# The way down of two chunks as seven block products over pairs of rows, with the third chunk first and in two parts

## The chip, the cores and the metric

The kernel runs on one core of one Trainium2 chip. Its time is the device time of one execution, in microseconds; a kernel is run several times and the median counts. One execution is also recorded by the hardware profiler. Engines are named as in the profile: PE is TensorE (PEld its weight loads), DVE is VectorE, ACT is ScalarE, POOL is GpSimd, SP is the engine that issues nearly all DMAs.

## The reference, cut to what matters

One layer of a streaming encoder, on 1024 + 128 = 1152 tokens of width 1024. The two feed-forward blocks (SwiGLU, inner width 2816) are what the change touches.

```python
def swiglu(x, w_gate, w_up, w_down):
    return (jax.nn.silu(x @ w_gate) * (x @ w_up)) @ w_down

def layer(x, ...):
    x = x + 0.5 * swiglu(rms_norm(x, norm_ffn1), w_ffn1_gate, w_ffn1_up, w_ffn1_down)
    m, ... = mixer(rms_norm(x, norm_mix), ...)      # gated DeltaNet heads and pooling heads, projected
    x = x + m
    x = x + 0.5 * swiglu(rms_norm(x, norm_ffn2), w_ffn2_gate, w_ffn2_up, w_ffn2_down)
    return x, ...
# after the layer: y = rms_norm(x, norm_final)
```

The data are float32. The kernel splits each operand of a large product into a high part (`float32r`) and a low part, so that one product takes three matmuls: high by high, high by low, low by high.

## The kernel before, in words

Tokens lie in the free dimension and features in the 128 partitions. There are three chunks of tokens: chunk 0 with 512, chunks 1 and 2 with 320 each. A feed-forward block is a `half_step` (gate and up) followed by `downs` (the way down). Between the two blocks stands the mixer, whose pieces of work are put in order by a list of names.

**gate_up.** A row `f` is one of the 22 blocks of 128 in the inner width. Chunk 0 takes plain products, 48 matmuls of 512 columns a row. Chunks 1 and 2 are taken together: gate and up are two block rows, the two halves of the width are the inner blocks, the two chunks are two block columns, and this 2 x 2 by 2 x 2 product is made from seven block products (B11, B21, T1, T2, T3, T4, B22) instead of eight, 84 matmuls of 320 columns a row. The sums of weights are made on POOL (`piece`, L314 and L318), a piece is cast on ACT (L319) and its low part made on DVE (L320). Pieces go round a ring of seven buffers, O0 to O6. The sums of activations are made once, by `operands`, into B0 to B6. There are three loops: for the first `AHEAD` = 9 rows chunk 0 goes alone, while the operands are made; rows 9 to 21 take all three chunks (the main loop); last, the first 9 rows are made up for chunks 1 and 2 (the last loop). Each row's result is split into two parts by `keep` (L337, L338) and written to `g_keep0`, `g_keep1` or `g_keep2` in DRAM.

**The way down.** `downs` takes the chunks in the order 1, 0, 2. A `Down` reads the 22 rows of its chunk back into A, B and x tiles (`fetch`, L618), and walks over units: one output block `d` of eight, with up to eight rows. A unit's weights are read into one of three R buffers (L171), cast (L182) and given a low part (L183) in one of three pairs of O buffers; each row is then three matmuls (L55) into PSUM. When all 22 rows of an output are in, DVE adds half of the sum to x (L534). In the second block, the final norm of chunk 1 runs beside chunk 0's way down, that of chunk 0 beside chunk 2's, and that of chunk 2 stands at the end: squares (L1362, L1368), two small sets of matmuls with a power on POOL between (L228, L229), a scaling on DVE or POOL (L1384, L1382), and the write of y (L1385).

**What sets the order.** The framework schedules instructions onto each engine's queue by the order in which they are written and by when it expects their operands and buffers to be ready; an instruction written later can so be put ahead. At run time each engine works through its queue in that fixed order and waits on semaphores. A buffer is named by a tag, and a new tile of a tag waits until the last use of the one before it. Reads of rows are put in a list (`pending`) and go out behind a weight read, so many at a time (`pace`), or all at once (`rest`).

Of the kernel before, what the change touches and what calls it, by code (L numbers as in the profile page):

```python
# [13 lines left out]
P = 128  # L14
# [10 lines left out]
CHUNKS = [(0, 512), (512, 320), (832, 320)]  # L25
HIST = 15
# [11 lines left out]
def trunk(ctx: ExitStack, tc: tile.TileContext, xin, s0, convst, poolst, cm_in, vec_in, small_in,  # L38
# [219 lines left out]

    STEPS = "B11 B21 T2 T1 T3 T4 B22".split()
    N = CHUNKS[1][1]  # L260
    N0 = CHUNKS[0][1]

    def operands(wi, op):
# [19 lines left out]
        split("B11", l1)  # L283
        V.tensor_sub(l1, l1, r1)
        yield
        split("T1", l1)
        yield
        split("B21", l2)
        V.tensor_sub(r1, r2, r1)
        yield  # L290
        split("B22", r2)
        yield
        V.scalar_tensor_tensor(r2, l1, -1.0, r2, ALU.mult, ALU.subtract)
        split("T2", r2)
        yield
        split("T3", r1)
        yield
        V.scalar_tensor_tensor(l2, r2, -1.0, l2, ALU.mult, ALU.subtract)
        split("T4", l2)
        yield  # L300

    def gate_up(wi, wg, wu, gk, H, RB, cs, ahead, norm, x0=None):


        gs, ring = Slots(), [0]

        def piece(*src, more=None):

            t = region(f"O{ring[0] % 7}", F32R)
            ring[0] += 1  # L310
            hi, lo = t[:, :512], t[:, 512:]
            if len(src) == 2:
                t = gs.get("s", 512)
                G.tensor_add(t, *src)  # L314
                src = [t]
            src = src[0]
            if more:
                G.tensor_add(more[0], src, more[1])  # L318
            A.copy(hi, src)  # L319
            V.tensor_sub(lo, src, hi.bitcast(F32))  # L320
            return [x.rearrange("p (k c) -> p k c", k=4) for x in (hi, lo)]

        def product(ps, w, hs, start=True, stop=True):
            for k in range(4):
                (whi, wlo), (hhi, hlo) = w, hs
                T.matmul(ps, whi[:, k, :], hhi[k], start=start and k == 0, stop=False, skip_group_check=True)
                T.matmul(ps, whi[:, k, :], hlo[k], start=False, stop=False, skip_group_check=True)
                T.matmul(ps, wlo[:, k, :], hhi[k], start=False, stop=stop and k == 3, skip_group_check=True)
# [7 lines left out]
        def keep(f, c, go, src):  # L336
            A.copy(go[:, 0], src)  # L337
            G.tensor_sub(go[:, 1], src, go[:, 0].bitcast(F32))  # L338
            SY.dma_start(gk[c][f].rearrange("p (s n) -> p s n", s=2), go.bitcast(F32))
# [3 lines left out]
        def gated0(f, pg, pu):  # L343
# [7 lines left out]
            keep(f, 0, go, sg)  # L351
            yield

        def temps():
            gs.place(region("x10"), ("p1", N, 2), ("c2", N, 2))
            gs.place(region("x11"), ("c3", N, 2), ("sum", 512, 1))
            for i in range(2):
                gs.place(region(f"x2{i}", F32R), ("go1", 2 * N, 1), ("go2", 2 * N, 1))

# [29 lines left out]
        def right_up(f, al, g1, u1, c2, c3):  # L389
# [4 lines left out]
            keep(f, 2, gs.get("go2", 2, N), c2)  # L394

        def left_up(f, al, w4, p1):
# [3 lines left out]
            keep(f, 1, gs.get("go1", 2, N), p1)  # L400
# [65 lines left out]
        for f in range(ahead, NF):  # L466
# [8 lines left out]
            next(done)  # L475
            c2 = right_gate(al, sm, g2, c3)
            product(pu, piece(u1), H0[0], True, False)
            right_up(f, al, g1, u1, c2, c3)
            w4 = piece(u2)
            product(pu, w4, H0[1], False, True)  # L480
            next(done)
            left_up(f, al, w4, p1)
# [4 lines left out]
        for f in range(ahead):  # L487
# [6 lines left out]
            if last:  # L494
                left_up(last[0], last[1], piece(last[2]), last[3])
            c2 = right_gate(al, sm, g2, c3)
            if f + 1 < ahead:
# [3 lines left out]
            last = f, al, u2, p1  # L501
        left_up(last[0], last[1], piece(last[2]), last[3])

    class Down:

        def __init__(self, c, wd, home):
            self.c, self.home = c, home
            fs = list(home)  # L510
            cuts = [(i, fs[i:i + 8]) for i in range(0, NF, 8)]

            self.units = []
            for ds in [(0, 1)] + [(d,) for d in range(2, KT)]:
                self.units += [(d, *cut) for cut in cuts for d in ds]
            self.next = ((wd[d], cut) for d, _, cut in self.units)
            self.raw = [fetch_unit(*next(self.next), 0) for _ in W["raws"]]

        def run(self, beside, done, most=1):
            c, home, ps = self.c, self.home, {}  # L520
            n = CHUNKS[c][1]
            beside = iter(beside)
            for d, at, cut in self.units:
                whi, wlo = split_unit(self.raw.pop(0))
                for src in self.next:
                    self.raw.append(fetch_unit(*src, most))
                    break
                if d not in ps:
                    ps[d] = pt("d")[:, :n]
                for i, f in enumerate(cut):  # L530
                    mm3(ps[d], whi[:, i, :], wlo[:, i, :], home[f][:, :n], home[f][:, n:], at + i == 0, at + i == NF - 1)
                next(beside, None)
                if at + len(cut) == NF:
                    V.scalar_tensor_tensor(xk(c, d), ps[d], 0.5, xk(c, d), ALU.mult, ALU.add)  # L534
                    if done:
                        done(d)
            for _ in beside:
                pass

    SPLITS = (("O1", "O2"), ("O3", "O4"), ("O5", "O6"))  # L540

    AHEAD = 9

    def half_step(wi, wg, wu, gk):
# [30 lines left out]
        rows = list(range(AHEAD, NF)) + list(range(AHEAD))  # L575
        fetch(1, gk, rows[:18], *[f"A{i}" for i in range(6)])
        for _ in run:
            pass
        fetch(1, gk, rows[18:], "A6", "B0")

    def downs(wd, gk, src, done=lambda c: None, after=lambda c: ()):
        weights(("R1", "R2", "R0"), SPLITS)
        rows = list(range(NF))
        d1 = Down(1, wd, homes[1])
        x_new(1)
        fetch_x(1, src)
        rest()
        fetch(0, gk, rows[:14], *[f"B{i}" for i in range(1, 7)], "x20", "x21")
        d1.run((), done(1))
        rest()  # L590
        fetch(0, gk, rows[14:], "A0", "A1", "A2", "A3")
        d0 = Down(0, wd, homes[0])
        fetch(2, gk, rows[:4], "B0")
        d0.run(after(1), done(0), 2)
        rest()
        fetch(2, gk, rows[4:], "B1", "B2", "B3", "B4", "B5")
        d2 = Down(2, wd, homes[2])
        x_new(2)
        fetch_x(2, src)
        for _ in range(4):  # L600
            pending.pop(0)()
        d2.run(after(0), done(2), 4)
        for _ in after(2):
            pass
# [3 lines left out]
    def fetch(c, gk, rows, *where):  # L608
# [4 lines left out]
        for tag in where:  # L613
            t = region(tag, F32R)
            for i in range(min(SIZE[tag] // n, len(left))):
                f = left.pop(0)
                out[f] = t[:, i * n:(i + 1) * n]
                pending.append(lambda f=f: SY.dma_start(out[f].bitcast(F32), gk[c][f]))  # L618
# [16 lines left out]
    weights(("R1", "R0", "O0"), SPLITS)  # L635
# [587 lines left out]
    rstd_of(0, pair(mt("raw", 512), mt("raw", 512), mt("Xs", 512)), R[0], False)  # L1223
# [129 lines left out]
    nt = Slots()  # L1353
    nt.place(region("Q"), ("nacc", 512, 1), ("nsq", 512, 1), ("r", 512, 2))
    squares = {}

    def square(c):

        def add(d):
            n = CHUNKS[c][1]  # L1360
            t = nt.get("nsq" if d else "nacc", n)
            A.activation(t, xk(c, d), AF.Square)  # L1362
            if not d:
                squares[c] = t
            elif c == 2 and d == KT - 1:
                squares[c] = [squares[c], t]
            else:
                V.tensor_add(squares[c], squares[c], t)  # L1368
        return add

    def final(c):
        o, n = CHUNKS[c]
        r = nt.get("r", n)
        last = c == 2
        pool = (2, 5) if last else (1, 4, 7)
        pr = yield from rstd_rest(n, squares[c], r)
        yield
        for k in range(KT):
# [7 lines left out]
            if not last:  # L1386
                yield

    downs(wd2, g_keep, x_keep, square, final)
# [90 lines left out]
```

## Time and profile before

| | |
|---|---|
| median of 3 runs | 2207.68 us (2204.58 to 2208.64) |
| profiled execution: time, and span from first to last instruction | 2208.91 us, 2207.1 us |
| granted clock of TensorE, mean | 0.996 |
| busy: PE / PEld / DVE / ACT / POOL | 98% / 89% / 60% / 41% / 28% |
| moved by DMA | 297.83 MB, 135 GB/s on the mean |
| first gate_up, first way down, mixer | about 0 to 527, 527 to 802, 802 to 1402 us |
| second gate_up, second way down, end | about 1402 to 1915, 1915 to 2194, 2194 to 2207 us |

In the profile's groups a line is one kind of instruction at one line of the kernel: engine, operation, tiles written and read, count, then busy time and mean duration, then the idle time of the engine just before and what ended it. "PEld" rows show weight loads, one for each matmul; as they overlap matmuls, a run of them without a break means that TensorE had work all along. A row of a window gives its length, then the busy time of each engine (with the count of instructions), the granted clock, the share of time in which the 16 DMA engines were busy and the rate.

### The profile page before, as it was taken

To read this page: it belongs to the slowest core of one execution; us is meant where nothing else is said; L and a number is where in the kernel's file an instruction comes from. 1 tells how busy PE (TensorE), PEld (TensorE's weight loads), DVE (VectorE), ACT (ScalarE), POOL (GpSimd) and SP (SyncE) were. 2 spreads that over 40 slices of the span, in tenths; PEclk is the share of its full clock that TensorE was granted. 3 is DMA by queue.
4 is the path that set the end of the run, shared out by engine and by line. 5 is a ranking of instruction groups with operands and counts; after the bars stand their busy time and mean duration, and the time that the engine had idled before them with its cause. 6 is when DMAs were issued, how large, how long until landed. Compare 5 with 4: busy or idle time off the path is not lost.

```text
span 2207.1 us, 32969 instructions
## 1 busy us (share of the span) xinstructions
PE 2155.4 (98%) x12599; PEld 1955.0 (89%) x12599; DVE 1333.2 (60%) x2329; ACT 909.1 (41%) x1726; POOL 614.5 (28%) x556
## 2 busy tenths in 40 slices
PE   8999999999999999999999998999999999999998
PEld 7899999999988987777989887888999999998898
DVE  7855555675423457778677867875555567543243
ACT  6433333453322345545544443543333345432232
POOL 1343443552000002322232333133434445300010
PEclk9999999999999999999999999999999999999999
DMA  6422232467753732122222123442322346676383
GB/s 250 143 94 88 91 112 91 153 197 270 245 188 118 249 110 62 51 65 58 86 63 80 44 92 92 136 151 89 108 87 91 113 144 188 226 259 225 95 291 103
DMA packets 103534, 297.83 MB, mean 135 GB/s; under 512 B 16336, under 2 KB 22352, under 8 KB 103120
## 3 DMA queue, kind: packets, MB, share of 16 engines
q1 hardware_dynamic: 103088, 295.40, 40.7%
q8 instruction: 99, 1.62, 0.3%
q14 instruction: 59, 0.48, 0.1%
q10 hardware_dynamic: 288, 0.33, 0.0%
HBM read 231.54 MB, written 64.14 MB: 134 GB/s over the span
## 4 chain that ended last, share of the span: by engine, by line
PE 86%; DVE 7%; issue 4%; ACT 1%; POOL 1%; DMA 1%; SPq 0%; DVEq 0%; ACTq 0%; POOLq 0%
PE ps_d L55 30%; PE ps_a L55 26%; PE ps_b L55 18%; PE ps_c L55 12%; DVE B L798 1%; DVE A L938 1%; DVE A L1140 1%; PE ps_b L59 1%; DVE A L937 1%; DVE O L183 0%; DMA R<-in_wd 0%; ACT O L182 0%; DVE B L941 0%; DVE R L935 0%; POOL A L1000 0%
## 5 line engine op out<-in xcount | busy, mean ns | idle before, releaser
L55 PE MATMUL ps_d<-B,O 128*128 128x320 f32 (+1 forms) x2784 | 503.6, 334 | 6.0 <-DVE x L819 3.0
L55 PEld LDWEIGHTS ps_d<-B,O 128*128 128x128 f32 x2784 | 441.5, 188 | 39.2 <-DVE x L819 5.2
L55 PE MATMUL ps_a<-A,O 128*128 128x512 f32 (+1 forms) x1712 | 390.8, 363 | 2.1 <-DVE A L938 1.6
L55 PE MATMUL ps_a<-B,O 128*128 128x320 f32 x2272 | 383.3, 309 | 0.0
L183 DVE TENSOR_TENSOR O<-R,O 128x1024 fp32r<-128x1024 f32 (+1 forms) x170 | 195.3, 1149 | 280.2 <-ACT O L182 276.2
L55 PEld LDWEIGHTS ps_a<-B,O 128*128 128x128 f32 x2272 | 348.6, 188 | 6.5 <-issue 0.2
L182 ACT CAST O<-R 128x1024 fp32r<-128x1024 f32 (+1 forms) x182 | 180.6, 993 | 403.9 <-PE ps_d L55 309.0
L55 PEld LDWEIGHTS ps_a<-A,O 128*128 128x128 f32 x1712 | 296.8, 191 | 37.9 <-issue 3.3
L320 DVE TENSOR_TENSOR O<-Q,O 128x512 fp32r<-128x512 f32 x180 | 156.9, 873 | 174.5 <-ACT O L319 174.4
L55 PE MATMUL ps_b<-A,O 128*128 128x512 f32 x1056 | 252.3, 393 | 7.2 <-ACT O L319 7.2
L55 PE MATMUL ps_d<-A,O 128*128 128x320 f32 (+1 forms) x1392 | 241.0, 331 | 1.0 <-DVE x L534 0.9
L55 PEld LDWEIGHTS ps_b<-A,O 128*128 128x128 f32 x1056 | 198.0, 189 | 47.0 <-ACT O L319 7.2
L55 PEld LDWEIGHTS ps_d<-A,O 128*128 128x128 f32 x1392 | 220.6, 188 | 16.4 <-issue 1.2
L320 DVE TENSOR_TENSOR O<-R,O 128x512 fp32r<-128x512 f32 x182 | 172.8, 952 | 34.6 <-ACT O L319 34.2
L319 ACT CAST O<-Q 128x512 fp32r<-128x512 f32 x180 | 111.3, 619 | 165.0 <-PE ps_b L55 66.9
L319 ACT CAST O<-R 128x512 fp32r<-128x512 f32 x182 | 112.3, 620 | 126.4 <-PE ps_a L55 64.3
L55 PE MATMUL ps_c<-A,O 128*128 128x512 f32 x624 | 151.2, 391 | 0.0
L55 PEld LDWEIGHTS ps_c<-A,O 128*128 128x128 f32 x624 | 115.0, 188 | 21.5
L338 POOL TENSOR_TENSOR x<-x,x 128x320 fp32r<-128x320 f32 x88 | 101.7, 1155 | 68.2 <-ACT x L337 65.9
L338 POOL TENSOR_TENSOR A<-A,A 128x512 fp32r<-128x512 f32 x44 | 72.2, 1640 | 122.0 <-ACT A L337 122.0
L314 POOL TENSOR_TENSOR Q<-R 128x512 f32<-128x512 f32 x36 | 51.5, 1430 | 162.1 <-DVE O L320 152.6
L229 POOL TENSOR_TENSOR rt<-rt,vec 128x3 f32<-128x3 f32 (+1 forms) x11 | 13.2, 1202 | 299.1 <-DVE rt L228 299.1
(282 smaller groups left out, 2705.6 us busy)
## 6 DMA issues: line engine op xcount, KB each, us to landing
R<-in_wd SPq DMA_DIRECT2D x80, 512.0 KB, 3.7
g_keep<-x SPq DMA_DIRECT2D x88, 320.0 KB, 2.3
R<-in_wu SPq DMA_DIRECT2D x49, 512.0 KB, 3.7
R<-in_wg SPq DMA_DIRECT2D x48, 512.0 KB, 4.1
g_keep<-A SPq DMA_DIRECT2D x44, 512.0 KB, 2.7
R<-in_wd SPq DMA_DIRECT2D x48, 384.0 KB, 3.7
B<-g_keep SPq DMA_DIRECT2D x46, 320.0 KB, 5.4
A<-g_keep SPq DMA_DIRECT2D x42, 320.0 KB, 4.2
```

The costliest lines, as they stand in the source:

```text
L55: self.put(nc.tensor.matmul(out, lhs, rhs, **k), n / 2400 + .003 if lhs.dtype == F32R else max(n, lhs.shape[-1]) / 600)
L59: self.put(nc.tensor.transpose(out, lhs, rhs), out.shape[-1] / 1200)
L182: A.copy(hi, raw)
L183: (e or V).tensor_sub(lo, raw, hi.bitcast(F32))
L314: G.tensor_add(t, *src)
L319: A.copy(hi, src)
L320: V.tensor_sub(lo, src, hi.bitcast(F32))
L338: G.tensor_sub(go[:, 1], src, go[:, 0].bitcast(F32))
L798: V.scalar_tensor_tensor(y[:, :512], raw[:, t:t + 512], cw[:, t:t + 1], y[:, :512], ALU.mult, ALU.add)
L937: V.tensor_tensor(tu[:, :n, :w], xrow(slice(None), m), Uc[:, :, m:m + 1].to_broadcast([P, n, w]), ALU.mult)
L938: V.tensor_tensor(Uc[:, :, m + 1:], Uc[:, :, m + 1:], tu[:, :n, :w], ALU.add)
L1140: V.tensor_tensor(buf[:, :, :have], cur[:, :, w_:w_ + have], cur[:, :, :have], ALU.add)
```

## The change

Chunks 1 and 2 now go down together, by the seven products that gate_up uses. An output pair is `d` and `d + 4` (two block rows), a pair of rows gives the two inner blocks, and the chunks are the two block columns. The 22 rows are 11 pairs in three groups of 4, 3 and 4 pairs; `ORDER` lays the weights out so that a group's even rows stand together, and then its odd ones. A unit of the new loop `down12` is a group and one of four output pairs: 12 units, numbered 0 to 11, with four weight blocks a11, a12, a21, a22 each. Each unit's partial results are added to x directly: five additions from PSUM on DVE, and two (p1, c3) by way of a copy on ACT and an addition on POOL. Weights come into four buffers (R0, R1, O5, O6), and pieces go round five (O3, O4, O0, O1, O2).

The operands (the right-hand sums) are made where the rows come from. In gate_up, rows from `AHEAD` = 8 on are collected in pairs; `combine` makes the four sums and seven splits of a pair and writes them to `g_keep2`. The first eight rows are written as they are to `g_keep1`; `downs` reads them back and makes their operands (group 0's, into B0 to B6) beside chunk 0's way down.

Chunk 0 goes first (`down0`), in two parts: all eight outputs over its first 14 rows, which are read during gate_up's last loop, and then over the other 8. The first and the last two outputs of each part are taken row by row together. The final norm of chunk 0 runs beside `down12`; those of chunks 1 and 2 both stand at the end. The numbers of some buffers change with this, in the mixer as well.

```diff
+GROUPS = [(0, 4), (4, 3), (7, 4)]
+ORDER = [2 * i + j for p, n in GROUPS for j in range(2) for i in range(p, p + n)]
...
+    def combine(l1, l2, r1, r2, put):
+        put("B11", l1)
+        V.tensor_sub(l1, l1, r1)
+        put("T1", l1)
+        put("B21", l2)
+        V.tensor_sub(r1, r2, r1)
+        put("B22", r2)
+        V.scalar_tensor_tensor(r2, l1, -1.0, r2, ALU.mult, ALU.subtract)
+        put("T2", r2)
+        put("T3", r1)
+        V.scalar_tensor_tensor(l2, r2, -1.0, l2, ALU.mult, ALU.subtract)
+        put("T4", l2)
...
+        def gated(f, c, t):
+            q, i = f // 2, 2 * (c - 1) + f % 2
+            if f < ahead:
+                SY.dma_start(gk[1][q][:, i * N:(i + 1) * N], t)
+                return
+            rows.setdefault(q, {})[i] = t
+            if len(rows[q]) < 4:
+                return
+            def put(name, src):
+                j = DOWN.index(name)
+                go = gs.get("go", 2, N)
+                A.copy(go[:, 0], src)
+                (V if name[0] == "B" else G).tensor_sub(go[:, 1], src, go[:, 0].bitcast(F32))
+                SY.dma_start(gk[2][q - ahead // 2][j].rearrange("p (s n) -> p s n", s=2), go.bitcast(F32))
+            sums.append(combine(*[rows[q][i] for i in range(4)], put))
...
+    def down12(wd, gk, op0, beside, done):
+        bl = Blocks(["O3", "O4", "O0", "O1", "O2"])
+        for tag in ("R0", "R1", "O5", "O6"):
+            gs.place(region(tag), ("raw", 1024, 1))
...
+        def fifth(g, d, w):
+            be, sm, c3 = pt("c")[:, :N], gs.get("sum", w[0].shape[-1]), gs.get("c3", N)
+            product(be, piece(w[2], w[3], more=(sm, w[0])), ops[g]["T1"], True, False)
+            A.mul(c3, be, -0.5)
+            G.tensor_add(xk(2, d + 4), xk(2, d + 4), c3)
+            return be, sm
...
+        ask(1, ["A5", "A0", "A1", "A2", "A3", "A4", "A6"])
+        for u, (g, d) in enumerate(units):
...
+            product(al, piece(a11), op["B11"])
+            A.mul(p1, al, 0.5)
+            G.tensor_add(xk(1, d), xk(1, d), p1)
+            product(ga, piece(a12), op["B21"])
+            if last:
+                left_low(*last)
+            if u == 4:
+                ask(2, [f"B{i}" for i in range(7)])
+            product(al, piece(sm), op["T2"], False)
+            add(1, d, ga)
+            add(2, d, al)
+            product(be, piece(sm, a12), op["B22"], False)
+            add(2, d, be)
+            if u + 1 < len(units):
...
+                w = load(g2, d2, 6 if g2 == 0 else 10)
+                nxt = w, fifth(g2, d2, w)
+            product(al, piece(a11, a21), op["T3"], False)
+            add(2, d + 4, al, -0.5)
...
-    AHEAD = 9
+    AHEAD = 8
...
-        fetch(1, gk, rows[:18], *[f"A{i}" for i in range(6)])
+        fetch(0, gk[0], ORDER[:14], *[f"A{i}" for i in range(7)])
...
+        down0(wd, [(home, first, 0), (second, ask, 2)], sums(), done0)
         rest()
-        d2.run(after(0), done(2), 4)
-        for _ in after(2):
-            pass
+        down12(wd, gk, op0, iter(after(0)), done12)
+        ends = [iter(after(c)) for c in (2, 1)]
```

In this cut some `yield` lines, the calls of the work beside (`next(beside, None)`) and of `ended` are left out. `ask(g, tags)` puts the reads of a group's operands on the list of pending reads; `load(g, d, most)` reads a unit's weights and lets `most` of the pending reads go behind them; `left_low` is the seventh product, T4, which is made one unit later.

More of the change, by code (lines that the diff above doesn't have):

```diff
@@ L282, in operands @@
                     yield
[L283 to L300, printed above, removed]
-    def gate_up(wi, wg, wu, gk, H, RB, cs, ahead, norm, x0=None):
[L305 to L328, printed above, removed]
+        yield from combine(l1, l2, r1, r2, split)
+    def gate_up(wi, wg, wu, gk, H, RB, cs, ahead, norm, x0=None):
+        bl = Blocks([f"O{i}" for i in range(7)])
+        gs, piece, product = bl.gs, bl.piece, bl.product
         def load(f, most=1):
@@ L350, in gated0 @@
             V.tensor_mul(sg, sg, su)
-            keep(f, 0, go, sg)
+            A.copy(go[:, 0], sg)
+            G.tensor_sub(go[:, 1], sg, go[:, 0].bitcast(F32))
+            SY.dma_start(gk[0][f].rearrange("p (s n) -> p s n", s=2), go.bitcast(F32))
             yield
         def temps():
[L355 to L358, printed above, removed]
+            gs.place(region("x10"), ("p1", N, 4))
+            gs.place(region("x11"), ("c2", N, 4))
+            gs.place(region("x20", F32R), ("go", 2 * N, 2))
+            gs.place(region("x21"), ("c3", N, 2), ("sum", 512, 1))
         def fifth(w):
@@ L393, in right_up @@
             V.tensor_mul(c2, c2, c3)
[L394 removed]
+            gated(f, 2, c2)
         def left_up(f, al, w4, p1):
@@ L501, in gate_up, with down0 @@
             last = f, al, u2, p1
+            step()
         left_up(last[0], last[1], piece(last[2]), last[3])
-    class Down:
-        def __init__(self, c, wd, home):
-            self.c, self.home = c, home
+    def down0(wd, parts, beside, done):
+        weights(("R0", "R1", "R2"), (("O4", "O5"), ("O6", "O0"), ("O1", "O2")))
+        units = []
+        for j, (home, ask, most) in enumerate(parts):
             fs = list(home)
[L511 to L531, printed above, removed]
@@ new lines, in down0, with more @@
+            at = sum(len(p[0]) for p in parts[:j])
+            cuts = [(i, fs[i:i + 8]) for i in range(0, len(fs), 8)]
+            for d in range(0, KT, 2):
+                pair = (d, d + 1)
+                both = d in (0, KT - 2)
+                us = [(e, i, cut) for i, cut in cuts for e in pair] if both else [(e, i, cut) for e in pair for i, cut in cuts]
+                units += [(j, e, at + i, i, cut, both) for e, i, cut in us]
+        todo = iter(units)
+        def more(most):
+            for j, d, o, i, cut, both in todo:
+                raw.append(fetch_unit(wd[d][:, o * P:(o + len(cut)) * P], most=most))
+                return
@@ new lines, in down0 @@
+        raw, ps, now = [], {}, -1
+        for _ in W["raws"]:
+            more(0)
+        left = list(units)
+        while left:
+            u = [left.pop(0)]
+            j, d, o, i, cut, both = u[0]
+            if both:
+                u.append(left.pop(0))
+            if j != now:
+                parts[j][1]()
+                now = j
+            home, _, most = parts[j]
+            ws = {}
+            for _, d, *_ in u:
+                ws[d] = split_unit(raw.pop(0))
+                more(most)
+                if i == 0:
+                    ps[d] = pt("d")[:, :N0]
+            for k, f in enumerate(cut):
+                for d, (whi, wlo) in ws.items():
+                    mm3(ps[d], whi[:, k, :], wlo[:, k, :], home[f][:, :N0], home[f][:, N0:], i + k == 0, i + k == len(home) - 1)
+            for d in ws:
@@ L532, in run @@
                 next(beside, None)
-                if at + len(cut) == NF:
-                    V.scalar_tensor_tensor(xk(c, d), ps[d], 0.5, xk(c, d), ALU.mult, ALU.add)
-                    if done:
+                next(beside, None)
+                if i + len(cut) == len(home):
+                    V.scalar_tensor_tensor(xk(0, d), ps[d], 0.5, xk(0, d), ALU.mult, ALU.add)
+                    if j == len(parts) - 1 and done:
                         done(d)
-            for _ in beside:
-                pass
@@ new lines, in downs, with first, sums, put @@
+    def downs(wd, gk, src, done0=None, after=lambda c: (), done12=None):
+        op0, stage = {}, []
+        def first():
+            for q in range(AHEAD // 2):
+                t = region(f"x{1 + q // 2}{q % 2}")
+                SY.dma_start(t, gk[1][q])
+                stage.append([t[:, i * N:(i + 1) * N] for i in range(4)])
+            for i, name in enumerate(DOWN):
+                t = region(f"B{i}", F32R)
+                op0[name] = [[t[:, (2 * k + s) * N:(2 * k + s + 1) * N] for k in range(4)] for s in range(2)]
+        def sums():
+            for q in range(AHEAD // 2):
+                def put(name, src):
+                    hi, lo = [op0[name][s][q] for s in range(2)]
+                    A.copy(hi, src)
+                    V.tensor_sub(lo, src, hi.bitcast(F32))
+                yield from combine(*stage[q], put)
+        home = dict(homes[0])
+        homes.clear()
+        second = {f: None for f in ORDER[14:]}
+        def ask():
+            fetch(0, gk[0], ORDER[14:], "A0", "A1", "A2", "A3")
+            second.update(homes[0])
+            rest()
+            for c in (1, 2):
+                x_new(c)
+                fetch_x(c, src)
+        down0(wd, [(home, first, 0), (second, ask, 2)], sums(), done0)
+        rest()
+        down12(wd, gk, op0, iter(after(0)), done12)
+        ends = [iter(after(c)) for c in (2, 1)]
+        while ends:
+            ends = [e for e in ends if next(e, e) is not e]
```

185 lines of the change are left out of this document (133 added, 52 removed).

## The prediction

> **What bounds the kernel now.** I read the page first, then busy times by stage, then the order in time of TensorE's weight loads.
>
> ```profile
> span 2207.1 us, 32969 instructions
> PE 2155.4 (98%) x12599; PEld 1955.0 (89%) x12599; DVE 1333.2 (60%) x2329; ACT 909.1 (41%) x1726; POOL 614.5 (28%) x556
> PE 86%; DVE 7%; issue 4%; ACT 1%; POOL 1%; DMA 1%; SPq 0%; DVEq 0%; ACTq 0%; POOLq 0%
> ```
>
> The chain of waits lies on TensorE for 86% of the span. A busy PE alone proves little, since ends of matmuls are modelled, so I look at the stages which the change touches:
>
> ```profile
> core 0: us, PE busy (x) PEld busy (x) DVE busy (x) ACT busy (x) POOL busy (x), PEclk, DMA share, GB/s
> 120.00:410.00 290.00, 290.00 (x1645) 265.57 (x1644) 159.10 (x212) 106.61 (x199) 117.67 (x86) 1.00 0.29 95
> 430.00:515.00 85.00, 85.00 (x582) 85.00 (x581) 63.37 (x92) 46.25 (x91) 47.39 (x39) 1.00 0.58 184
> 526.80:802.20 275.40, 274.38 (x1582) 253.30 (x1581) 104.58 (x118) 82.41 (x94) 2.21 (x4) 1.00 0.62 207
> 1914.90:2194.40 279.50, 277.68 (x1609) 256.25 (x1609) 112.64 (x126) 84.08 (x103) 12.47 (x10) 1.00 0.62 209
> ```
>
> The rows are the main loop of the first gate_up (all three chunks), its last loop (chunks 1 and 2 by seven products), and the two ways down. TensorE is without a gap in the first two and has 1 to 2 us of gaps in each of the last two, at a granted clock of 1.00. So matmuls taken out of the ways down shorten the kernel one for one, as long as the new loop is fed. The price of one:
>
> ```profile
> 724.67 77.56 PEld L55 LDWEIGHTS ps_d<-B,O 128*128 128x128 f32 x528
> 1484.76 5.44 PE ps_a L55 x24
> 547.00 9.24 PEld L55 LDWEIGHTS ps_d<-A,O 128*128 128x128 f32 x63 [1.16 <-issue]
> 547.03 9.48 PE L55 MATMUL ps_d<-A,O 128*128 128x320 f32 x63 [0.93 <-DVE x L534]
> 2140.17 54.26 PEld L55 LDWEIGHTS ps_d<-B,O 128*128 128x128 f32 x370 [2.09 <-DVE O L183]
> ```
>
> The whole way down of chunk 2 is one unbroken run: 77.56/528 = 0.147 us for a matmul of 320 columns. With 512 columns it is 5.44/24 = 0.227. The last three rows are the main stalls of the ways down, 1.2 us in the first, 2.1 in the second.
>
> **The change part by part.** *Matmuls.* Chunks 1 and 2 cost 2 x 8 x 22 x 3 = 1056 matmuls in each way down; seven products for 4 output pairs over 11 row pairs cost 7 x 4 x 11 x 3 = 924. Chunk 0 keeps its 528. Over both ways 264 go: 264 x 0.147 = **-38.8 us**. gate_up keeps its matmuls; only the split of rows between its loops moves (8 and 14 for 9 and 13).
>
> *Feeding the new loop.* One unit (a group and an output pair) has 84 matmuls, 12.3 us; the 3-pair group has 63, 9.3 us. Its other work has the shapes of gate_up's last loop:
>
> ```profile
> L320 DVE TENSOR_TENSOR O<-Q,O 128x512 fp32r<-128x512 f32 x26 | 21.9, 843 | 10.8 <-ACT O L319 10.8
> L319 ACT CAST O<-Q 128x512 fp32r<-128x512 f32 x25 | 15.5, 619 | 13.8 <-PE ps_d L55 7.7 <-PE ps_a L55 5.4 <-PE ps_b L55 0.7
> L314 POOL TENSOR_TENSOR Q<-x,R 128x512 f32<-128x512 f32 x4 | 5.2, 1302 | 2.8 <-DVE O L320 2.8
> L338 POOL TENSOR_TENSOR x<-x,x 128x320 fp32r<-128x320 f32 x14 | 12.4, 883 | 17.1 <-ACT x L337 17.1
> L399 DVE SCALAR_TENSOR_TENSOR x<-ps_a,x 128x320 f32<-128x320 f32 x7 | 3.3, 477 | 0.0
> L364 ACT ACTIVATE x<-ps_c 128x320 f32<-128x320 f32 x7 | 3.1, 438 | 5.0 <-PE ps_c L55 5.0
> L393 DVE TENSOR_TENSOR x<-x,x 128x320 f32<-128x320 f32 x7 | 8.4, 1194 | 0.2
> ```
>
> DVE: 7 low parts x 0.84 + 5 additions from PSUM x 0.48 = 8.3 us of 12.3. ACT: 7 x 0.62 + 2 x 0.44 = 5.2. POOL: 4 sums x 1.30 + 2 additions x 0.88 = 7.0. gate_up's last loop carries 75%, 54% and 56% on these engines (row 430 to 515) and TensorE waits nowhere. The one thing that is tighter here is the ring of split pieces, 5 buffers for 7: a piece can be made once the product five before it ended, so four products, 7.0 us, cover a cast, a low part and the sum ahead of them (2.8 us). I take **+2** for both ways, from 0 to 12 (0.07 us for each of 168 products).
>
> *DMA.* Weights fall from 72 to 48 units a way, of up to 512 KB for the old and two of 384 or 512 KB for the new. The operands come as 49 reads of 320 KB and 4 of 640 KB in place of 44 rows. What matters is when: group 2's 28 operands (9.2 MB) go into the B tiles that group 0 frees, so between the starts of units 4 and 8, with the weights of units 5 to 8 (3.4 MB) between them on SP's one queue. That is 12.6 MB.
>
> ```profile
> 540.00:570.00 30.00, 28.98 (x197) 28.48 (x196) 12.88 (x14) 9.63 (x10) 0.00 (x0) 1.00 1.01 381
> 600.00:620.00 20.00, 20.00 (x103) 17.44 (x102) 6.54 (x9) 4.85 (x7) 0.00 (x0) 1.00 0.88 316
> R<-in_wd SPq DMA_DIRECT2D x80, 512.0 KB, 3.7
> g_keep<-x SPq DMA_DIRECT2D x88, 320.0 KB, 2.3
> ```
>
> With a full queue 381 GB/s went through, so the 12.6 MB take 33 us. Unit 8's first product starts 3 x 9.3 + 5 x 1.3 = 34 us after unit 4 and wants its weights 2.8 us earlier, at 31.5, and the weight reads stand behind ten operand reads each. If the first of them waits 1 us for its slot, TensorE loses about 2.5 us: **+5** for both, from 0 to 17 (at the 316 GB/s of the second row 40 us are needed, 8.4 a way late). "DMA: Bandwidth & Descriptors" of the Trainium skill (Specifications) gives a core about 358 GB/s of HBM. The trace went above that, at 381, and the measurement decides; by 358 the estimate of the term would be about +9 and the sum 4 us higher.
>
> *The start of the new loop.* Unit 1's weights go into O5 and O6, and O6 is free only when chunk 0 ends; the reads (3.7 us in flight), two POOL sums and a split then stand against 5 products, 8.8 us. **+1** for both, 0 to 8. Should SP keep the written order at the start of a way, chunk 0's fourth weight unit would queue behind the four 640 KB reads, which wait for gate_up's last row to be written (2.3 us): some 4 us a way.
>
> ```profile
> 517.86 0.42 SPq L174 DMA_DIRECT2D O<-in_win  x1
> 523.06 0.44 SPq L618 DMA_DIRECT2D B<-g_keep  x1
> ```
>
> It does not keep it: a weight of the mixer, written far behind, went out ahead of this way's rows, since its buffer was free. I cost that at nothing; the first two units (16 x 3 x 0.227 = 10.9 us) are the cover.
>
> *Chunk 0 in two parts.* 8 more PSUM evacuations on DVE cost nothing by themselves; 104.58 us in 275.40 leave room, also for 16 additions and 28 splits of the first group's operands. But pairs of outputs now run row by row together and end 0.7 us apart, where both PSUM buffers are wanted at once: three such edges a way. The one of before cost 0.93 (row 547.03); I take 0.3 each, **+2** for both ways, 0 to 5.5.
>
> *gate_up's sums.* For every two rows 4 additions and 3 low parts come onto DVE, at the 1.19 of L393 at worst 8.4 us in 46.6; it had 159.10 in 290.00, 55%, and comes to 73%, as the last loop has with TensorE full. ACT gets 1.5 casts a row. Cover is there; **+1**, 0 to 8.
>
> *Stalls that go.* The three rows above: **-2.5**, 0 to -3.6.
>
> *The end.* Now two chunks of 320 finish together:
>
> ```profile
> 2194.74 0.49 DVE L534 SCALAR_TENSOR_TENSOR x<-ps_d,x 128x320 f32<-128x320 f32 x1 [7.60 <-PE ps_d L55]
> 2200.50 2.84 DVE L1384 SCALAR_TENSOR_TENSOR x<-x,vec,ps_d 128x320 f32<-128x320 f32 x6 [3.19 <-ACT Q L234]
> 2201.08 3.13 SPq L1385 DMA_DIRECT2D out_y<-x  x6
> ```
>
> Six more scalings and six more writes on SP, 3.1 us, less the 1.8 us of chunk 1's last product, which runs when chunk 2 is done: 1.3; I take **+2**, 1.3 to 5. The mixer's start keeps its cover: A0 to A3 are free one group (49 us) ahead.
>
> *Sum.* -38.8 + 2 + 5 + 1 + 2 + 1 - 2.5 + 2 = -28.3. The profiled execution took 2208.91 (its span and 1.8 around it), so 2180.6; it lies 1.2 above the median of the runs, from which I get 2179.4. **Forecast 2180.**
>
> **The rivals.** *The queue takes part of the gain.* Group 1 runs at the speed of its reads: that term at +17 and the start at +4 give 2180 + 12 + 3 = 2195. For it: one queue, ten reads ahead of each weight; share 1.01 at such times before. Against: the shortage is one stage of 37 us.
>
> *Evacuations ahead of pieces (slower).* In a unit an addition that waits for product k's end is written ahead of the low part of product k+1, on the same DVE. Were that the order on the engine, five products of seven would wait 0.48 + 0.84 less the two matmuls that need no low part (0.29), 1.0 us: 120 products, +124 us, 2304. Queued behind would be the next low parts, and TensorE for them. It decides from 28/120 = 0.24 us a product. Against: gate_up's last loop is written alike and shows 85.00 of 85.00. For: 5 buffers let the engines run less far ahead.
>
> *DVE and POOL block each other (slower).* Each low part (0.68 by itself, 0.84 on the mean) would wait for a whole POOL sum of 1.30: 7 x 2.0 + 2.4 = 16.4 us, DVE the bound, about +4 in 24 units, 2276. This is the exclusive lock on the shared port that "SBUF — State Buffer" of the Trainium skill (Who interferes with whom) states. Against: gate_up's last loop has the same mix, so what blocking there is lies in its means already; the rows show how little, 0.92 beside a POOL sum and 0.68 without.
>
> ```profile
> 448.64 1.30 POOL L318 TENSOR_TENSOR x<-Q,R 128x512 f32<-128x512 f32 x1 [1.12 <-issue]
> 449.57 0.92 DVE L320 TENSOR_TENSOR O<-Q,O 128x512 fp32r<-128x512 f32 x1 [0.22 <-ACT O L319]
> 454.13 0.68 DVE L320 TENSOR_TENSOR O<-Q,O 128x512 fp32r<-128x512 f32 x1
> ```
>
> *The change does not do what it says in time.* gate_up's additions hold up its low parts by 1 us a row, 28 rows in both main loops: what the ways down gain is given back, 2208. Against: 73%.
>
> **How the numbers follow.** Forecast (2168 to 2188) 0.63; the queue (2188 to 2203) 0.20; given back 0.04; evacuations 0.10; port 0.03. Under 0.2%, 4.4 us, no difference can be told. Faster 0.63 + 0.20 = 0.83, same 0.04, slower 0.13. The lowest sum of the terms is -38.8 + 1.3 - 3.6 = -41, 2168; the upper end takes in the queue's rival, 2203.
>
> **What would show it.** 924 matmuls of 320 columns between chunk 0's end and the end of each way, at 0.147 each: about 136 us. TensorE's gaps there name the wait: DMA of R or O from in_wd before units 6 to 8 is the queue, DVE with O is the order of evacuations, low parts above 1.2 us on the mean the port. gate_up's rows should still take 85.00 in 85.00 and 290.00 in 290.00. The forecast is wrong if gaps of the new loop exceed 15 us a way, or if gate_up or the mixer's start grows by more than 10.

## The result

The changed kernel takes 2213.28 us (median of 7 runs, 2211.89 to 2218.47) against 2207.68 before (7 runs, 2204.02 to 2208.91): 1.0032 times as long, 95% interval 1.0020 to 1.0043. Slower by 0.3%, where 2180 was forecast. The profiled execution took 2211.95 us.

From the page of the changed kernel, the span, the engines' busy times and the chain by engine:

```profile
span 2210.2 us, 33211 instructions
PE 2134.5 (97%) x12341; PEld 1922.0 (87%) x12341; DVE 1519.3 (69%) x2685; ACT 937.0 (42%) x1905; POOL 734.0 (33%) x667
PE 78%; DVE 10%; issue 3%; POOL 3%; DMA 3%; ACT 2%; DVEq 0%; SPq 0%; POOLq 0%; ACTq 0%
```

TensorE lost 258 matmuls (12,599 to 12,341 in the records; some can be missing) and is busy 20.9 us less, yet the span is 3.1 us longer. Its share of the chain went from 86% to 78%, and DVE, POOL and DMA now hold pieces of it. By stages (busy time of PE, PEld, DVE, ACT, POOL, then the granted clock, the DMA share and GB/s), in the same stretches as shown before, with each way down also cut where chunk 0 ends:

```profile
120.00:410.00 290.00, 290.00 (x1652) 266.18 (x1651) 191.06 (x258) 110.81 (x218) 108.86 (x89) 1.00 0.33 117
430.00:515.00 85.00, 85.00 (x582) 85.00 (x581) 66.62 (x93) 42.04 (x83) 37.83 (x29) 1.00 0.61 202
526.80:648.50 121.70, 121.00 (x528) 97.93 (x527) 51.72 (x77) 31.01 (x48) 5.06 (x3) 1.00 0.54 180
648.50:802.60 154.10, 140.77 (x915) 135.70 (x914) 108.24 (x165) 68.47 (x130) 84.18 (x71) 0.99 0.52 177
1917.30:2039.90 122.60, 120.97 (x528) 97.99 (x527) 56.22 (x82) 35.80 (x56) 5.06 (x3) 1.00 0.53 179
2039.90:2194.00 154.10, 143.66 (x946) 140.81 (x945) 110.92 (x163) 64.89 (x129) 87.70 (x73) 0.98 0.49 171
```

gate_up is as it was: no gap in the two stretches, and the way down begins at 526.8 as before. The new loop takes 154.1 us in each way. Its 924 matmuls at 0.147 are 135.7, so some 18 us a way are lost there, 37 in all, nearly the 38.8 that the change had taken out. A way down with its chunk 0 took 275.4 and 279.5 before and takes 275.8 and 276.7 now; what lies between the two ways grew by 2.0, the end (from the last product to the end of the span) from 12.7 to 16.2. That is +0.4 + 2.0 - 2.8 + 3.5 = +3.1, the difference of the spans. The 2.0 lie in the mixer: from its first up product of chunk 0 on (at 1405.64 before, 1408.04 now), the second gate_up takes 509.4 us in both. Why the mixer takes longer was not looked at.

Not all of the 37 us are gaps. TensorE's own gaps in the two rows are 13.3 and 10.4 us. In three places (743 to 747, 2064 to 2068 and 2163 to 2167 us) the granted clock fell to 0.5 behind a stall: 24 matmuls whose loads take 3.52 us elsewhere took 5.05 and 4.96 in the last two places, in all some 5 us of the 37. It does not come behind every stall: after 2.23 us at 789.49 the loads took 3.52, after 2.38 at 2163.61 they took 4.96, and no run here shows what decides it. The second way's loop also holds matmuls of chunk 0's final norm, which wait 2.1 us for a power on POOL.

**Where the new loop waits.** First the sums of the waits in the first way down (engine and line, what it waited for: us in total, times, longest):

```profile
PEld ps_a L58 <- ACT O L287: 8.8, 6, 2.2
...
PE ps_a L58 <- DVE x L653: 7.8, 6, 2.0
...
POOL Q L282 <- DMA R<-in_wd: 10.0, 3, 4.9
POOL Q L282 <- DMA O<-in_wd: 8.3, 3, 5.4
...
DVE O L288 <- ACT O L287: 23.7, 9, 4.3
DVE x L653 <- POOL x L678: 13.6, 8, 2.0
```

TensorE's matmuls into ps_a wait for DVE's additions to x (L653), which must read a sum before the next product goes into its buffer. The profile puts nearly the same stalls of the weight loads down to a cast of a piece (L287; L288 makes its low part), but the order in time below shows that the addition ended later. DVE waits for casts, and for POOL's addition of p1 (L678). POOL's sums of weights (L282) wait for weights from HBM, up to 5.4 us at a time. The order in time of one such wait, in unit 2 of the first way (units counted from 0; start and length in us, engine and line, operation, and in brackets the idle time before and what ended it; the rows of this chain alone):

```profile
675.32 0.67 DVE L288 TENSOR_TENSOR O<-O,O 128x512 fp32r<-128x512 f32 x1
676.02 0.33 SPq L641 DMA_DIRECT2D O<-in_wd  x1
...
678.06 0.44 ACT L677 ACTIVATE R<-ps_a 128x320 f32<-128x320 f32 x1 [1.09 <-PE ps_a L58]
...
679.82 1.30 POOL L282 TENSOR_TENSOR Q<-O 128x512 f32<-128x512 f32 x1 [5.38 <-DMA O<-in_wd]
681.08 1.30 POOL L282 TENSOR_TENSOR Q<-R,R 128x512 f32<-128x512 f32 x1
...
682.34 1.75 POOL L286 TENSOR_TENSOR Q<-Q,O 128x512 f32<-128x512 f32 x1
...
684.05 0.88 POOL L678 TENSOR_TENSOR x<-x,R 128x320 f32<-128x320 f32 x1
684.89 1.30 POOL L282 TENSOR_TENSOR Q<-Q,O 128x512 f32<-128x512 f32 x1
684.96 0.49 DVE L653 SCALAR_TENSOR_TENSOR x<-ps_b,x 128x320 f32<-128x320 f32 x1 [2.03 <-POOL x L678]
685.37 1.36 DVE L288 TENSOR_TENSOR O<-Q,O 128x512 fp32r<-128x512 f32 x1
...
686.66 0.48 DVE L653 SCALAR_TENSOR_TENSOR x<-ps_a,x 128x320 f32<-128x320 f32 x1
687.06 0.68 DVE L288 TENSOR_TENSOR O<-O,O 128x512 fp32r<-128x512 f32 x1
687.66 0.48 DVE L653 SCALAR_TENSOR_TENSOR x<-ps_a,x 128x320 f32<-128x320 f32 x1
...
688.25 3.52 PEld L58 LDWEIGHTS ps_a<-B,O 128*128 128x128 f32 x24 [1.69 <-ACT O L287]
688.28 3.75 PE L58 MATMUL ps_a<-B,O 128*128 128x320 f32 x24 [1.45 <-DVE x L653]
...
689.33 0.68 DVE L288 TENSOR_TENSOR O<-R,O 128x512 fp32r<-128x512 f32 x1
...
690.03 0.33 SPq L641 DMA_DIRECT2D R<-in_wd  x1
...
693.35 1.01 POOL L282 TENSOR_TENSOR Q<-R 128x384 f32<-128x384 f32 x1 [4.89 <-DMA R<-in_wd]
```

To be read as a ring. A unit's weights fill two of the four buffers R0, R1, O5 and O6, so the second read for a coming unit can go out only when the last piece of the unit two back, a22, has been split: the low part ends at 675.99, the read goes out at 676.02. It lands at 679.8, and the sum on POOL that needs it stood there for 5.38 us. Behind that sum stand, in order, two more sums and the addition of p1. ScalarE had evacuated p1 of this unit at 678.06; its addition to x is fourth in POOL's queue and runs at 684.05. DVE's next addition writes the same x tile and waits for it; behind this addition on DVE stand a low part and two more additions. TensorE's next product is T3, which is added to the sum that the last of these additions reads. Its low part, the row at 685.37, ends at 686.73, that addition at 688.14, and the matmuls start at 688.28, after 1.45 us (1.69 by the weight loads). Being late itself, this unit splits its own a22 late, at 689.33, and the next read goes out at 690.03: the lateness is handed on. From read to read are 14.0 us, where a unit's 84 matmuls take 12.3.

### The profile page after: what moved, and what is told of

The parts are those of the page before. It is cut to its first block, busy times and chain, and to the rows that moved or that the text cites. A ratio compares the mean times of both kernels' runs of the same rounds, so it can differ in the third digit from the quotient of the medians.

```text
span 2210.2 us, 33211 instructions
## 1 busy us (share of the span) xinstructions
PE 2134.5 (97%) x12341; PEld 1922.0 (87%) x12341; DVE 1519.3 (69%) x2685; ACT 937.0 (42%) x1905; POOL 734.0 (33%) x667
## 4 chain that ended last, share of the span: by engine, by line
PE 78%; DVE 10%; issue 3%; POOL 3%; DMA 3%; ACT 2%; DVEq 0%; SPq 0%; POOLq 0%; ACTq 0%
PE ps_a L58 28%; PE ps_b L58 19%; PE ps_d L58 17%; PE ps_c L58 13%; DVE O L288 2%; DMA R<-in_wd 1%; DVE B L982 1%; DVE O L186 1%; DVE A L1122 1%; DVE x L653 1%; PE ps_b L62 1%; DVE A L1324 1%; POOL Q L282 1%; POOL A L282 1%; POOL x L678 1%
## 5 line engine op out<-in xcount | busy, mean ns | idle before, releaser
L58 PE MATMUL ps_a<-A,O 128*128 128x320 f32 (+1 forms) x1952 | 426.4, 354 | 3.1 <-DVE A L1122 1.6
L288 DVE TENSOR_TENSOR O<-Q,O 128x512 fp32r<-128x512 f32 (+1 forms) x238 | 216.5, 913 | 193.6 <-ACT O L287 189.6
L58 PE MATMUL ps_b<-A,O 128*128 128x512 f32 (+1 forms) x1128 | 263.8, 388 | 7.4 <-ACT O L287 7.4
L58 PE MATMUL ps_d<-A,O 128*128 128x512 f32 x1056 | 244.1, 391 | 2.3 <-DVE x L602 1.4
L287 ACT CAST O<-Q 128x512 fp32r<-128x512 f32 (+1 forms) x238 | 143.2, 604 | 187.6 <-POOL Q L282 47.5
L288 DVE TENSOR_TENSOR O<-R,O 128x512 fp32r<-128x512 f32 (+1 forms) x216 | 200.3, 931 | 32.5 <-ACT O L287 31.8
L58 PE MATMUL ps_d<-B,O 128*128 128x320 f32 (+1 forms) x1104 | 205.2, 331 | 5.4 <-DVE x L1003 3.7
L282 POOL TENSOR_TENSOR Q<-R 128x512 f32<-128x512 f32 (+1 forms) x44 | 58.4, 1328 | 433.2 <-DVE O L288 149.0
L287 ACT CAST O<-R 128x512 fp32r<-128x512 f32 (+1 forms) x216 | 130.9, 611 | 134.5 <-PE ps_a L58 54.5
L58 PE MATMUL ps_c<-A,O 128*128 128x512 f32 (+1 forms) x816 | 186.9, 377 | 1.1 <-DVE O L288 1.1
L58 PEld LDWEIGHTS ps_d<-B,O 128*128 128x128 f32 x1104 | 171.2, 189 | 16.0 <-DVE x L1003 6.1
L185 ACT CAST O<-R 128x1024 fp32r<-128x1024 f32 (+1 forms) x86 | 85.9, 1010 | 183.0 <-PE ps_d L58 136.5
L58 PE MATMUL ps_c<-B,O 128*128 128x320 f32 x912 | 145.8, 310 | 3.0 <-DVE O L288 1.9
L186 DVE TENSOR_TENSOR O<-R,O 128x1024 fp32r<-128x1024 f32 (+1 forms) x74 | 87.4, 1188 | 50.3 <-ACT O L185 29.7
```

Source lines behind the costliest of these rows:

```text
L58: self.put(nc.tensor.matmul(out, lhs, rhs, **k), n / 2400 + .003 if lhs.dtype == F32R else max(n, lhs.shape[-1]) / 600)
L185: A.copy(hi, raw)
L186: (e or V).tensor_sub(lo, raw, hi.bitcast(F32))
```

## The experiments

The ratios are to the kernel before in the same sessions (2206.97 to 2207.71). What is said of gains against the change sets medians of two sessions beside each other.

**1 and 2. Cutting the ring at either of two places.** The first makes both POOL additions on DVE, straight from PSUM:

```diff
-            A.mul(c3, be, -0.5)
-            G.tensor_add(xk(2, d + 4), xk(2, d + 4), c3)
+            add(2, d + 4, be, -0.5)
...
-            A.mul(p1, al, 0.5)
-            G.tensor_add(xk(1, d), xk(1, d), p1)
+            add(1, d, al)
```

> Edit: the two additions that go by way of ACT and POOL (p1 after B11, c3 after T1) become DVE additions straight from PSUM, so DVE waits for nothing that stands in POOL's queue. Theory 'chain through POOL' (a POOL sum that waits for late weights holds the p1 addition behind it, DVE's next addition waits for that, and the low part of T3 stands behind): the 1.7 to 2.2 us gaps of most units of four pairs go, the new loop falls from 154 us to about 142 a way, the time from 2213 to about 2190. Theory 'weights late by themselves' (the slot is free too late): gaps stay, 2213 within 4, perhaps 1 us a unit worse since DVE has 0.96 us more a unit. Theory 'mixer and group 2 reads': gaps before unit 7 stay too.

Measured: 2191.47, ratio 0.9932 (0.9918 to 0.9947), 21.8 us less than the change.

The second gives the weights a fifth buffer (the squares that lay in R3 go to a new tile E0, which also takes a small tile of the mixer):

```diff
-        for tag in ("R0", "R1", "O5", "O6"):
+        for tag in ("R0", "R1", "O5", "O6", "R3"):
...
-    wab = const.tile([P, KT, 16], F32R, tag="wab", name="wab")
+    wab = region("E0", F32R)[:, :KT * 16].rearrange("p (k c) -> p k c", c=16)
...
-            nt[0].place(region("R3"), ("nacc", 512, 1), ("nsq", 512, 1))
+            nt[0].place(region("E0"), ("nacc", 512, 1), ("nsq", 512, 1))
```

> Edit: five weight buffers instead of four in the new loop (R3 added; the squares of chunk 0 and one small mixer tile move to a new tile of their own). The read of unit u+1 then waits for the T3 sum of unit u-1 and no more for its a22 split. Theory 'weights late by themselves' and theory 'chain through POOL' both say that the gaps of 1.7 to 2.2 us go, since the late weights start the chain: about 2190. Theory 'order of evacuations' (5 buffers of pieces, DVE behind PSUM waits, whatever the weights): gaps stay, 2213 within 4.

Measured: 2193.01, ratio 0.9939 (0.9922 to 0.9955), 20.3 us less. Neither edit changes a matmul or a byte that is read. The first also takes two instructions a unit off POOL, which the last section shows to hold up low parts on DVE; the second leaves POOL's work as it is and gains nearly as much, so that cannot be the whole of it.

**3. Both.**

> Both edits, five weight buffers and the two additions on DVE. If weights and chain are one cause: as the better of the two alone, about 2190. If each has gaps of its own: lower than either, about 2180, the new loop near 138 us a way.

Measured: 2184.02, ratio 0.9898 (0.9884 to 0.9913), 29.3 us less than the change. The two gains (21.8 and 20.3) do not add, as is to be expected of two cuts in one ring. From first to last product the new loops take 142.6 us (648.55 to 791.16) and 141.8 (2024.24 to 2166.08), where about 138 was expected; that is 24 of the 29 us. The stretch that the first loop filled in the change, which here takes in some 11 us of the mixer:

```profile
648.50:802.60 154.10, 148.78 (x980) 143.10 (x980) 133.36 (x213) 69.86 (x123) 59.09 (x50) 1.00 0.53 181
```

65 matmuls more are done in it than in the change; DVE's work rose from 108.24 to 133.36, 87% of the time, and TensorE waits less all the same. DVE's load was not what held the loop up.

**4. The queue.** Group 2's operands are not read; the kernel multiplies by group 0's instead, which leaves out 28 reads a way and computes another sum.

```diff
-                ask(2, [f"B{i}" for i in range(7)])
+                ops[2] = op0
```

> Edit: the 28 reads of group 2's operands are left out; group 2's products use group 0's operands, so both ways down compute another sum. Theory 'the queue' (group 2's 9.2 MB of reads delay the weights of units 5 to 8): units 4 to 8 lose their gaps, some 7 us in the first way and 4 in the second, time about 2202; units 0 to 3 and 9 to 11 keep theirs. If the reads are not the cause: 2213 within 3.

Measured: 2215.92, ratio 1.0044 (1.0028 to 1.0061): no gain. The stretch of group 1, in which these reads run, first of the change, then of this kernel, and last of kernel 3, which does read them:

```profile
700.00:740.00 40.00, 38.75 (x261) 37.94 (x259) 29.94 (x50) 19.72 (x41) 24.77 (x23) 1.00 0.92 337
```

```profile
700.00:740.00 40.00, 38.48 (x259) 37.75 (x258) 26.90 (x46) 18.43 (x39) 25.89 (x24) 1.00 0.35 111
```

```profile
700.00:740.00 40.00, 40.00 (x275) 40.00 (x274) 36.87 (x60) 20.52 (x38) 17.67 (x16) 1.00 0.76 276
```

At 337 GB/s TensorE has 1.25 us without work in 40, at 111 GB/s 1.52. With the ring cut and the reads kept, it has no gap at all, with DVE at 36.87 of 40. The queue costs nothing. The reads for which POOL waits go out late because no buffer is free, not because others stand ahead of them.

**5. One of the two additions.** Only p1's goes to DVE (the second hunk of experiment 1).

> Of the two additions that POOL does in each unit, only p1's (B11's product) goes to DVE straight from PSUM; c3's stays on ScalarE and POOL. Theory (chain through POOL's queue): p1's addition is the one that stands behind the T1 sum which waits for the next unit's weights, and DVE's next addition waits for p1's; so moving it alone brings most of what moving both brought: 2193, from 2190 to 2198. Rival (POOL is late by its load, either addition counts the same): half of the 22 us, 2202.

Measured: 2199.92, ratio 0.9967 (0.9957 to 0.9977). That is 13.4 of the 21.8 us, between the two expectations and in the range of neither. p1's addition carries the larger part, and c3's counts too; by which way c3's does was not tried.

**6. Chunk 0 without pairs.** Kernel 3, with chunk 0's outputs one at a time:

```diff
-                both = d in (0, KT - 2)
+                both = False
```

> Both additions on DVE and the fifth weight buffer, as in e3_both (2184), and chunk 0's way down with each output run by itself throughout, no pairs row by row. Theory (the edges where a pair ends together cost 2 to 3 us of each way's 121.7 and 122.6): 121.7 comes to about 120 in both, in all 2180. Rival (the rows or the first weights are late and the pairs give them time): the part's beginning waits instead, 2184 or up to 2188.

Measured: 2175.02, ratio 0.9868 (0.9851 to 0.9885): 9.0 us less than kernel 3, more than either theory gave, and the fastest of all. TensorE's weight loads in chunk 0's stage (count, busy us and mean ns, then idle us before them and what ended it), first of the change, first and second way:

```profile
L58 PEld LDWEIGHTS ps_d<-A,O 128*128 128x128 f32 x525 | 97.9, 188 | 23.7 <-ACT O L185 1.4 <-issue 1.1 <-DVE O L186 0.9
L58 PEld LDWEIGHTS ps_d<-A,O 128*128 128x128 f32 x525 | 97.9, 188 | 24.6 <-issue 2.5 <-ACT O L185 1.3 <-DVE O L186 0.8
```

and of this kernel:

```profile
L58 PEld LDWEIGHTS ps_d<-A,O 128*128 128x128 f32 x525 | 98.3, 188 | 21.4 <-DMA A<-g_keep 1.1
L58 PEld LDWEIGHTS ps_d<-A,O 128*128 128x128 f32 x525 | 98.4, 188 | 20.5
```

Some 20 us of idle is there in any case, since a load of 0.188 goes with a matmul of 0.227 (525 x 0.039 = 20.5). Above that the change waits 3.2 and 4.1 us; 2.3 and 2.1 of its waits are put down to L185 and L186, the cast and the low part of chunk 0's weights; a pair run row by row wants both outputs' split weights at once. (For the rest the profile mostly names nothing.) With single outputs these waits are gone, and 0.9 us is left in the first way, for a row of g_keep.

**7. The same on the change alone.** The edit of experiment 6, nothing else.

> The change as it is, with chunk 0's outputs one at a time throughout: the pairs row by row are the only thing taken out. If what e6_single gained over e3_both (9 us) is the edges of the pairs, it comes here too, whatever the new loop waits for: 2204 to 2206, of it 2 to 3 us in each way's stage of chunk 0 and 2 in the first units of the second way's new loop. Rival (the earlier start of the new loop is lost again where its first units wait for weights that come no earlier): 2209 to 2213.

Measured: 2203.26, ratio 0.9984 (0.9975 to 0.9994), 10.0 us less than the change. So the edges are a loss of their own, and the two add: 29.3 + 10.0 = 39.3, against 38.3 for kernel 6. With this alone the change would have come out 0.16% faster than before. Where the 10 us are, by TensorE's rows of this kernel where the first new loop, the second way's chunk 0 and the second new loop begin (start and length):

```profile
646.69 1.92 PE L58 MATMUL ps_c<-B,O 128*128 128x320 f32 x12
...
1912.95 119.19 PE L58 MATMUL ps_d<-A,O 128*128 128x512 f32 x525
2031.97 1.92 PE L58 MATMUL ps_c<-B,O 128*128 128x320 f32 x12
```

and the same places of the change:

```profile
648.71 1.92 PE L58 MATMUL ps_c<-B,O 128*128 128x320 f32 x12
...
1917.47 19.08 PE L58 MATMUL ps_d<-A,O 128*128 128x512 f32 x81
...
2040.10 1.92 PE L58 MATMUL ps_c<-B,O 128*128 128x320 f32 x12
```

At the first new loop it is 2.0 us ahead, at the second way's chunk 0 4.5, at the second new loop 8.1. So 2.0 and 3.6 us are won by the end of the two stages of chunk 0, and 2.5 between them, in the first new loop and the work up to the second way. The two profiled executions are 8.9 us apart, so little comes after.

**8. The mixer's preparation.** In kernels 3 and 6 the first way still loses some 4 us in its units 8 and 9. There ScalarE and DVE scale and split chunk 0 for the mixer. Writing that work one tile a step was tried first, on kernel 3:

```diff
-    downs(wd1, g_keep, xin)
+    downs(wd1, g_keep, xin, after=lambda c: ahead_of_mix(c) if c == 0 else ())
...
-    hb = {0: h_tiles(0)}
-    scale_split(0, 1, *hb[0])
+    hb = early
```

> As e3_both, and in the first way down the scaling and splitting of chunk 0's tiles for the mixer, which came in one stretch on ScalarE and DVE when group 1 ends, is written one tile a step over the last units. Theory (this stretch holds up the casts and low parts of units 8 and 9, 2.5 and 2 us): TensorE's two gaps there shrink below 1 us each, 2180. Rival (the pieces there wait for weights or operands of group 2, not for the mixer's work): the gaps stay, 2184.

Measured: 2185.24, ratio 0.9907 (0.9892 to 0.9923), no gain. It decides nothing: on ScalarE and DVE these instructions stand, all but one, where they stood, between the same pieces. So the next kernel, built on 6, gives them a factor that comes late:

```diff
-    scale_split(0, 1, *hb[0])
+    V.scalar_tensor_tensor(late, xk(2, 1)[:, :KT], 0.0, vec[:, 8:16], ALU.mult, ALU.add)
+    for k in range(KT):
+        A.mul(hb[0][0][k], xk(0, k), late[:, k:k + 1])
+        V.scalar_tensor_tensor(hb[0][1][k], xk(0, k), late[:, k:k + 1], hb[0][0][k].bitcast(F32), ALU.mult, ALU.subtract)
```

> As e6_single (2175), and the mixer's scaling and splitting of chunk 0 takes its factors from a copy that is made only when unit 9's second output is written, so that these 16 instructions come two units later on ScalarE and DVE. Theory (they hold up the pieces of units 8 and 9 in the first way, 3.7 and 0.8 us lost there): units 8 and 9 take 12.3 each, and at most 2 us come back in units 10 and 11, in all 2171 to 2173. Rival (POOL's sums of unit 9 come late for their weights or temporaries, whatever DVE does): the 16.0 and 13.1 us of these units stay, 2175 or more.

Measured: 2177.07, ratio 0.9861 (0.9845 to 0.9877), the same as kernel 6 within the intervals. The weight loads of kernel 6, then of this one:

```profile
745.62 5.07 PEld L58 LDWEIGHTS ps_a<-B,O 128*128 128x128 f32 x24 [2.60 <-ACT O L287]
```

```profile
742.86 3.56 PEld L58 LDWEIGHTS ps_a<-B,O 128*128 128x128 f32 x24
...
771.49 5.05 PEld L58 LDWEIGHTS ps_a<-B,O 128*128 128x128 f32 x24 [2.39 <-issue]
```

The stall of kernel 6 in unit 8, 2.60 us of waiting and 5.07 for loads that take 3.56 undisturbed, is gone; it comes back in unit 10, 2.39 and 5.05, where the mixer's work now stands. So that work is its cause, and it costs some 4 us wherever it meets this loop; moving it gains nothing. The 1.5 us by which the loads are longer are the clock: it was granted at 0.67 in both stretches. (The expectation that little would come back was wrong.)

**9. The end.** The kernel with 8's first edit, with 8 of the last 16 writes on ScalarE's queue instead of 4:

```diff
-            (A if last and k in pool else SY).dma_start(y_out[:, o * KT + k * n:o * KT + (k + 1) * n], x)
+            (A if last and k in (1, 2, 4, 5) else SY).dma_start(y_out[:, o * KT + k * n:o * KT + (k + 1) * n], x)
```

> As e7_spread, and four of the last twelve writes of y for chunks 1 and 2 each go out on ScalarE's queue instead of SP's. Theory (after the last product SP writes 12 tiles in 6.9 us, and its queue sets the end): 3 us less than e7_spread, 2177. Rival (the scalings on DVE ahead of the writes set the end, or ScalarE's issue comes as late): the same as e7_spread, 2180.

Measured: 2186.09, ratio 0.9909 (0.9890 to 0.9929): no gain over 2185.24. Its end:

```profile
2173.97 7.20 SPq L1579 DMA_DIRECT2D out_y<-x  x8
2173.39 1.47 DVE L1578 SCALAR_TENSOR_TENSOR x<-x,vec,ps_d 128x320 f32<-128x320 f32 x3 [0.93 <-ACT A L237]
2175.64 4.21 DVE L1578 SCALAR_TENSOR_TENSOR x<-x,vec,ps_d 128x320 f32<-128x320 f32 x9 [0.78 <-ACT A L237]
```

Eight writes on SP take 7.2 us, where twelve took 6.93 in the change, so the length of SP's queue is not what sets the end. What is left is the work ahead of the writes, of which twelve scalings on DVE take 5.7 us with a pause between the chunks; no run shortened them.

## Why the prediction was wrong

**The matmuls.** The count was right, 264 fewer at 0.147 us. The chunks 1 and 2 of a way would take 135.7 us if fed.

**The step that failed: feeding the new loop**, taken as +2 us for both ways, 0 to 12 at most. The loops lost 37 us in all, of which experiment 3 won back 24 (and 5 outside them). By time lost, 18 us a way, that is over the mark of 15 that the prediction set itself; TensorE's gaps alone, 13.3 and 10.4, are not. The step looked at the ring of five pieces and at the engines' loads, which were in fact light (DVE 108 of 154 us, POOL 84), and compared them with gate_up's last loop. It did not look at the raw weights: four buffers are two units, so a read is tied to the split of the unit before last. Nor did it ask what stands behind the sum that waits for this read on POOL. The additions on POOL, 0.88 each, were counted as load. Each is a link between two in-order queues: POOL waiting for a transfer holds up DVE, and DVE holds up TensorE. gate_up's last loop, which had such work and no gap, showed that the engines can do it, not that this loop's buffers let them: it has five raw buffers (one in Q, and R0 to R3), which is what experiment 2 gave the new loop.

**Chunk 0 in two parts**, +2 with 0 to 5.5: it cost 10 (experiment 7). The term asked when both PSUM buffers are wanted at once, and such waits were there: 0.24 us in the first way, 0.24 and 0.93 in the second. The larger part are the waits for both outputs' split weights and what the new loops lost behind them, which the term did not have. How the pairs cost the first new loop time was not followed.

**The start of the new loop**, +1: 0.3 us in unit 0 of the first way. The first stall of size, 1.76 us at 674.27 in unit 1, is the ring's.

**DMA**, +5: nothing (experiment 4). The reads do fit, at 337 GB/s in the stretch of group 1.

**gate_up's sums**, +1: nothing, 290.00 of 290.00 and 85.00 of 85.00, with DVE at 66% and 78%. **Stalls that go**, -2.5, were not measured by themselves. With experiments 3 and 6 the sum of the other terms holds. Without the feeding (+2) and the edges (+2) it gives 2176.6 on the profiled basis, and kernel 6 took 2175.1 in its profiled execution. That agreement is partly chance, since the mixer's preparation (experiment 8) is not in the sum and the queue's +5 is.

**The end**, +2 with 1.3 to 5: +3.5, inside its bounds. The six more writes on SP were counted; experiment 9 shows that their number is not what sets it.

**The rivals.** The queue (2195) was refuted. "Evacuations ahead of pieces" named the place: an addition on DVE with low parts queued behind it. But the addition waits for POOL's addition to the same x tile, not for a product of TensorE, and DVE waits 13.6 us for it in the first way, where the rival took 62 us a way from TensorE. When these additions were all put on DVE the loop became faster, which is the opposite of what that rival fears. "Given back" (2208) is nearest in time and wrong in place, since gate_up gave nothing back. "DVE and POOL block each other" (2276) had low parts above 1.2 us on the mean as its sign; the 54 of 128x512 in the first new loop took 0.91. The blocking itself is real (last section), at a smaller price.

## What to carry to other kernels

When a product is replaced by fewer ones with more preparation, count every ring of buffers in the loop, the raw inputs' included: how many units ahead may a read go, and what must have ended before it is issued. On an in-order engine, ask of each instruction that can wait for a transfer what stands behind it, and whether another engine waits for that; a cheap addition there can cost more than its time. A loop that shows no gap proves that the engines can carry its mix, and says nothing of a loop with fewer buffers.

## What the runs showed of the hardware

A low part on DVE that begins inside a POOL sum does not run beside it. In the wait shown above POOL's sum runs from 684.89 for 1.30, and the low part that began at 685.37 ends at 686.73, 0.54 after it; undisturbed it takes 0.68. Two more, from the kernel of experiment 8's second edit:

```profile
735.63 1.30 POOL L282 TENSOR_TENSOR A<-R,O 128x512 f32<-128x512 f32 x1 [0.63 <-DVE O L288]
735.87 1.61 DVE L288 TENSOR_TENSOR O<-A,O 128x512 fp32r<-128x512 f32 x1
...
746.46 1.63 POOL L286 TENSOR_TENSOR A<-A,R 128x512 f32<-128x512 f32 x1 [4.09 <-issue]
747.25 1.39 DVE L288 TENSOR_TENSOR O<-A,O 128x512 fp32r<-128x512 f32 x1
```

Both low parts end 0.55 us after the POOL sum. "SBUF — State Buffer" of the Trainium skill (Who interferes with whom) states that a DVE instruction with two SBUF inputs contends with a GpSimd instruction that reads SBUF, and that the port pair they share is an exclusive lock. These rows agree, and the rival built on it was waved off on a misread row. The prediction took a low part of 0.92 beside a POOL sum as a sign of little blocking. That row says the same as these: the sum ended at 449.94 and the low part at 450.49, 0.55 later; it was short only because it began late in the sum. What the blocking costs this kernel was not tried by itself.
